# An encoder trunk on one core: the feed-forward's products in one matmul of 512 columns and one of 256, and adaLN columns taken at other places

## The chip, the cores and the metric

The kernel runs on one core of a Trainium2 chip. The metric is the device time of one execution in microseconds; the median of three runs before the change is 2146.71 us (2144.97 to 2148.68).

The engines: TensorE (PE) multiplies a stationary 128x128 weight block with up to 512 moving columns and adds into PSUM, VectorE (DVE) and ScalarE (ACT) do the elementwise work, GpSimd (POOL) a few small powers, and SyncE (SP) issues the DMAs, all on one queue. PSUM has eight banks of 512 fp32 columns in each of 128 partitions.

## The reference

Two layers over 256 tokens of width 2048. Layer 0 mixes tokens by a gated MLP, layer 1 by grouped-query attention; behind each stands a gated convolutional feed-forward. Each sub-layer is normed, and shifted, scaled and gated by columns made from a conditioning vector (adaLN):

```python
cond = silu(c)
for i in range(2):
    sh1, sc1, gt1, sh2, sc2, gt2 = split(cond @ w_ada[i] + b_ada[i], 6)
    h = rmsnorm(x, g_norm[i, 0]) * (1 + sc1) + sh1
    x = x + gt1 * (gmlp(h) if i == 0 else gqa(h))
    h = rmsnorm(x, g_norm[i, 1]) * (1 + sc2) + sh2
    x = x + gt2 * conv_ffn(h)
return rmsnorm(x, g_final)

def conv_ffn(h):                     # w_up: 2048 x 11264, w_down: 5632 x 2048
    a = h @ w_up
    a = conv_w[0]*shift(a, 1) + conv_w[1]*a + conv_w[2]*shift(a, -1) + conv_b
    g, val = split(a, 2)
    return (gelu(g) * val) @ w_down
```

Everything is fp32.

## The kernel before, in words

Activations stand transposed: 16 blocks `x[:, j, :]` of 128 features by 256 tokens. An fp32 product is made of three products of a shorter format. A weight tile (1 MB, 128x2048, by DMA) is cast on ACT into `hi` (line 188), and DVE makes the rest `lo` = w - hi (line 189), 1024 columns at a time. Activations have the same two parts, `hhi`/`hlo` for a sub-layer's input (lines 276, 277) and `fhi`/`flo` for the gated products (284, 285). `prod_b` (line 208) issues three matmuls of 256 columns into one place of PSUM: hi with hhi, hi with hlo, lo with hhi. I call these three a triple; all go through `mm` in line 205. `hi` and `lo` have five buffers each, the raw tiles five, shared by weights and adaLN columns. A whole bank holds two halves of 256 tokens: block i of the gate and its partner.

A feed-forward (`ffn`) goes through these stages. `outer` with `pfa`: seven blocks of gate and value, input blocks 0 to 7, all held at once in seven banks; their sums are parked in `part`. `pfc`: the next seven blocks over all 16 input blocks. Then `up_rest` (tile `pf`, blocks 0 to 6): the other eight input blocks, 16 triples, added to `part` (line 659). Then `up_pair` (tile `pf`, blocks 14 to 43): two weight tiles and 32 triples each. Each finished block goes to `epilogue`: two identities with scale on ACT (610), four shifted taps on DVE (613), a gelu on ACT (615), a product (616), and the split into `fhi`/`flo`. The hidden width is taken in three parts of 16, 16 and 12 blocks; behind each stands the down product `wdn` (tile `pd`): for each of 16 output blocks j, 16 or 12 triples, and a `residual` (line 291) that adds gate times sum to `x[:, j]`. In the first layer the first part is parked (`A.copy`, line 703) and added later.

An adaLN column (`ada`, line 140) is a 1 MB DMA and a DVE multiply with row sum over 128x2048; there are 192. They wait in a list. `weight` calls `pump`, which adds the stage's rate to a credit and takes a column from the list for each whole credit; `need` takes all up to one that is wanted now. The rates are `RK` for the four stages of `outer` and what follows in each layer, `RU` and `RD` in the first feed-forward's `up_pair` and `wdn`, `RW` in the attention's output product. The epilogues are not issued at once but appended to `pend`, and go when the next weight tile is issued. A scheduler then sets each engine's order by its own estimates.

After the feed-forward of layer 0 a mean square is taken (`pm_mx`, `r_mx`) on PE, DVE and POOL, then the attention's first product `pk`, 512 moving columns with the activation as the other operand, three for each pair.

## Time and profile before

| | |
|---|---|
| median of three runs | 2146.71 us |
| the profiled execution | 2148.5 us |
| its span | 2146.7 us |
| TensorE's granted clock, mean | 0.985 of 2.4 GHz |
| busy DVE, ACT | 1703.8 us, 1018.3 us |
| HBM read | 575.99 MB, 269 GB/s over the span |

A profile is one execution. Busy time is counted for each engine by itself; matmuls are pipelined, so a matmul's own 0.28 us overlaps the next, and the time it costs is the distance from start to start. The same holds on DVE and ACT to a smaller degree: I call the distance a step. The stages by their first matmuls: gated MLP to 330 us, first feed-forward 338 to 1095 us, attention 1101 to 1370 us, second feed-forward from 1380 us.

### The profile page before, as it was taken

To read this page: it belongs to the slowest core of one execution; us is meant where nothing else is said; L and a number is where in the kernel's file an instruction comes from. 1 tells how busy PE (TensorE), PEld (TensorE's weight loads), DVE (VectorE), ACT (ScalarE), POOL (GpSimd) and SP (SyncE) were. 2 spreads that over 40 slices of the span, in tenths; PEclk is the share of its full clock that TensorE was granted. 3 is DMA by queue.
4 is the path that set the end of the run, shared out by engine and by line. 5 is a ranking of instruction groups with operands and counts; after the bars stand their busy time and mean duration, and the time that the engine had idled before them with its cause. 6 is when DMAs were issued, how large, how long until landed. Compare 5 with 4: busy or idle time off the path is not lost.

```text
span 2146.7 us, 39158 instructions
## 1 busy us (share of the span) xinstructions
PE 2081.6 (97%) x16348; PEld 2026.0 (94%) x16348; DVE 1703.8 (79%) x2258; ACT 1018.3 (47%) x1484; POOL 17.4 (1%) x15
## 2 busy tenths in 40 slices
PE   6899998999999999999999999899999999999997
PEld 6778998999999999999988789899999999999997
DVE  7998999899988999889986687866978666655665
ACT  3435433446544554345445654444653445434542
POOL 0000000000000000000000000000000000000000
PEclk8999999999999999999999999899999999999999
DMA  9998898985888889988966456678558655555542
GB/s 394 404 370 331 307 382 320 366 334 214 302 343 330 331 331 330 344 323 314 338 230 225 139 196 236 217 273 310 184 194 319 231 178 192 181 190 184 182 157 95
DMA packets 85137, 580.62 MB, mean 270 GB/s; under 512 B 9952, under 2 KB 11488, under 8 KB 25056
## 3 DMA queue, kind: packets, MB, share of 16 engines
q1 hardware_dynamic: 84528, 577.93, 72.8%
q8 instruction: 128, 2.10, 0.4%
q14 instruction: 49, 0.40, 0.0%
q10 hardware_dynamic: 432, 0.20, 0.0%
HBM read 575.99 MB, written 2.10 MB: 269 GB/s over the span
## 4 chain that ended last, share of the span: by engine, by line
PE 51%; issue 37%; DVE 7%; ACT 2%; DMA 2%; POOL 0%; SPq 0%; POOLq 0%; DVEq 0%; ACTq 0%
PE pf L205 18%; PE pd L205 12%; PE po L205 4%; DVE ada L140 3%; PE pw L205 3%; PE pk L205 3%; DVE lo L189 3%; PE pq L205 3%; PE pfc L205 3%; PE pfa L205 2%; PE pub L205 1%; ACT hi L188 1%; DMA w<-in_wu 1%; PE pqo L549 1%; DMA ada<-in_wada 1%
## 5 line engine op out<-in xcount | busy, mean ns | idle before, releaser
L188 ACT CAST hi<-w 128x1024 fp32r<-128x1024 f32 x740 | 739.5, 1009 | 892.0 <-PE pf L205 353.8
L189 DVE TENSOR_TENSOR lo<-w,hi 128x1024 fp32r<-128x1024 f32 x740 | 857.4, 1169 | 323.1 <-ACT hi L188 319.8
L205 PE MATMUL pf<-hhi_f,hi 128*128 128x256 f32 x2144 | 604.3, 282 | 0.0
L205 PE MATMUL pf<-hhi_f,lo 128*128 128x256 f32 x2144 | 601.1, 280 | 0.0
L205 PE MATMUL pf<-hlo_f,hi 128*128 128x256 f32 x2144 | 600.9, 280 | 0.0
L140 DVE CUSTOM_DVE_ANT_0 ada<-ada,cond_bc,bada 128x2048 f32<-128x2048 f32 x192 | 449.6, 2346 | 37.0 <-DMA ada<-in_wada 36.9
L205 PEld LDWEIGHTS pf<-hlo_f,hi 128*128 128x128 f32 x2144 | 404.8, 189 | 0.0
L205 PEld LDWEIGHTS pf<-hhi_f,lo 128*128 128x128 f32 x2144 | 404.3, 189 | 0.0
L205 PEld LDWEIGHTS pf<-hhi_f,hi 128*128 128x128 f32 x2144 | 403.8, 188 | 0.0
L205 PE MATMUL pd<-fhi_f,lo 128*128 128x256 f32 x1408 | 394.7, 282 | 0.0
L205 PE MATMUL pd<-flo_f,hi 128*128 128x256 f32 x1408 | 393.3, 280 | 0.0
L205 PE MATMUL pd<-fhi_f,hi 128*128 128x256 f32 x1408 | 391.5, 279 | 0.2 <-ACT hi L188 0.2
L205 PEld LDWEIGHTS pd<-fhi_f,hi 128*128 128x128 f32 x1408 | 264.9, 189 | 0.4 <-ACT hi L188 0.4
L205 PEld LDWEIGHTS pd<-fhi_f,lo 128*128 128x128 f32 x1408 | 264.6, 188 | 0.2
L205 PEld LDWEIGHTS pd<-flo_f,hi 128*128 128x128 f32 x1408 | 264.5, 188 | 0.0
L205 PE MATMUL pfc<-hlo_f,hi 128*128 128x256 f32 x448 | 123.4, 283 | 1.6 <-DVE hlo_f L277 1.6
L205 PE MATMUL pfc<-hhi_f,hi 128*128 128x256 f32 x448 | 123.3, 283 | 1.1 <-ACT hi L188 1.1
L205 PE MATMUL pfc<-hhi_f,lo 128*128 128x256 f32 x448 | 113.8, 282 | 0.0
L613 DVE SCALAR_TENSOR_TENSOR t<-pf,cw,t 128x255 f32<-128x255 f32 x240 | 102.2, 475 | 0.0
L205 PEld LDWEIGHTS pfc<-hlo_f,hi 128*128 128x128 f32 x448 | 85.3, 190 | 2.0 <-DVE hlo_f L277 2.0
L205 PEld LDWEIGHTS pfc<-hhi_f,hi 128*128 128x128 f32 x448 | 85.1, 190 | 1.3 <-ACT hi L188 1.3
L205 PEld LDWEIGHTS pfc<-hhi_f,lo 128*128 128x128 f32 x448 | 79.9, 190 | 0.2 <-DVE lo L189 0.2
(194 smaller groups left out, 2809.5 us busy)
## 6 DMA issues: line engine op xcount, KB each, us to landing
ada<-in_wada SPq DMA_DIRECT2D x192, 1024.0 KB, 6.5
w<-in_wup SPq DMA_DIRECT2D x134, 1024.0 KB, 4.9
w<-in_wdn SPq DMA_DIRECT2D x64, 1024.0 KB, 4.9
w<-in_wup SPq DMA_DIRECT2D x48, 896.0 KB, 6.2
w<-in_wdn SPq DMA_DIRECT2D x32, 768.0 KB, 4.3
w<-in_wu SPq DMA_DIRECT2D x16, 1024.0 KB, 7.9
w<-in_wv SPq DMA_DIRECT2D x16, 1024.0 KB, 7.2
w<-in_wout SPq DMA_DIRECT2D x16, 1024.0 KB, 6.8
```

The costliest lines, as they stand in the source:

```text
L140: V.tensor_tensor_reduce(out=w, in0=w, in1=cond_bc, op0=ALU.mult, op1=ALU.add, scale=1.0, scalar=bada[:, l, m:m + 1], accum_out=mod[:, l, ...
L188: A.copy(hi[:, :n], w[:, c:c + n])
L189: V.tensor_tensor(out=lo[:, :n], in0=w[:, c:c + n], in1=hi[:, :n].bitcast(F32), op=ALU.subtract)
L205: T.matmul(out, lhsT=a, rhs=b, start=start, stop=stop, skip_group_check=True)
L549: T.matmul(po, lhsT=va[:, kc, g * P:(g + 1) * P], rhs=ps_[h][:, kc, :], start=kc == 0, stop=kc == TC - 1)
L613: V.scalar_tensor_tensor(out=o[:, to], in0=a[:, frm], scalar=cw[:, l, tap, n:n + 1], in1=o[:, to], op0=ALU.mult, op1=ALU.add)
```

## The change

`hhi`/`hlo` become the two halves of one tile `hh`, and `fhi`/`flo` of one tile `f`, so that both parts of an activation are 512 columns in a row. A new `prod_w` issues a matmul of `hi` with all 512 columns into a whole bank and one of `lo` with the first 256 into its first half: two matmuls for three. It is used by `up_rest`, `up_pair` and `wdn`; `outer` keeps `prod_b`. The two halves of a bank are then still to be summed. `up_pair` does this with an ACT copy of one half and a DVE sum into `ab` (function `whole`), `up_rest` with a second sum into `part`, `wdn` with a second residual, the parked part with a copy and a sum for two output blocks at once. PSUM is cut into four tiles of two banks instead of eight of one; `pfa` and `pfc` put two blocks into one tile, `wdn` two output blocks j. The rates change as the diff shows: the first attention stages get rates of their own (`RP`, `RQ`, the second set before the keys are rotated). In SP's order 138 columns are issued ahead of the attention's first weight tile instead of 160, and all 192 ahead of the first `wdn` of the second feed-forward instead of 183. The program's lines move by 2 in `mm`, and by up to 32 in `ffn`.

```diff
 HS = 20
-RK = ((0.75, 0.75, 0.75, 0.0), (0.6, 0.6, 0.6, 0.0))
-RU = 0.75
-RD = 0.85
-RW = 0.5
+RK = ((0.75, 0.75, 0.75, 0.0), (0.9, 0.9, 0.9, 0.5))
+RU = 0.55
+RD = 0.6
+RP = 0.5
+RQ = 0.5
+RW = 0.75
 RB = 5
...
     def bank(name, tag=None):
-        return cur["ps"].tile([P, 512], F32, tag=tag or cur["tag"], name=name, bufs=cur["bufs"][tag or cur["tag"]])
-    def phase(stack, name, nf, bufs={"ps": 8}, tag="ps", rt="ps"):
+        return cur["ps"].tile([P, cur["bw"]], F32, tag=tag or cur["tag"], name=name, bufs=cur["bufs"][tag or cur["tag"]])
+    def phase(stack, name, nf, bufs={"ps": 8}, tag="ps", rt="ps", bw=512):
...
                                                      space=bass.MemoryType.PSUM, reuse_waits="tile"))
-        cur["bufs"], cur["tag"], cur["rt"] = bufs, tag, rt
+        cur["bufs"], cur["tag"], cur["rt"], cur["bw"] = bufs, tag, rt, bw
         cur["f"] = stack.enter_context(tc.tile_pool(name=name + "_f", bufs=nf, reuse_waits="tile"))
...
         mm(out, wlo, xhi, False, stop)
+    def prod_w(out, w, xx, start, stop):
+        whi, wlo = w
+        mm(out, whi, xx, start, False)
+        mm(out[:, :S], wlo, xx[:, :S], False, stop)
...
     def new_h(name, step=0):
-        hts["hi"] = hbuf.tile([P, NB, S + step], F32R, tag="hhi", name=f"hhi_{name}")[:, :, :S]
-        hts["lo"] = hbuf.tile([P, NB, S + step], F32R, tag="hlo", name=f"hlo_{name}")[:, :, :S]
+        hts["x"] = hbuf.tile([P, NB, 2 * S + step], F32R, tag="hh", name=f"hh_{name}")
+        hts["hi"], hts["lo"] = hts["x"][:, :, :S], hts["x"][:, :, S:2 * S]
         return hts["hi"], hts["lo"]
...
     def split_f(name, src):
-        fbuf = cur["f"]
-        fhi = fbuf.tile([P, S + STEP], F32R, tag="fhi", name=f"fhi_{name}")[:, :S]
-        flo = fbuf.tile([P, S + STEP], F32R, tag="flo", name=f"flo_{name}")[:, :S]
+        f = cur["f"].tile([P, 2 * S + STEP], F32R, tag="f", name=f"f_{name}")
+        fhi, flo = f[:, :S], f[:, S:2 * S]
         A.copy(fhi, src)
         V.tensor_tensor(out=flo, in0=src, in1=fhi.bitcast(F32), op=ALU.subtract)
-        return fhi, flo
+        return fhi, flo, f[:, :2 * S]
...
+            state["rate"] = RP
             pk = [[bank(f"pk{t}_{n}", ("pb", "pa", "pb")[n]) for n in range(3)] for t in range(TC)]
...
         with ExitStack() as st:
-            ff = phase(st, f"ff{l}", FB)
+            ff = phase(st, f"ff{l}", FB, {"ps": 4}, bw=1024)
             R = rstd()
             hhi, hlo = new_h(f"f{l}", STEP)
+            hx = hts["x"][:, :, :2 * S]
             yacc = ff.tile([P, NB, S], F32, tag="yacc", name="yacc")
...
                 return b[:, :S], b[:, S:]
+            def banks(name):
+                two = [bank(f"{name}_{i}") for i in range((KO + 1) // 2)]
+                return [two[i // 2][:, (i % 2) * 512:(i % 2 + 1) * 512] for i in range(KO)]
+            def both(b):
+                v = b.rearrange("p (s h c) -> p s h c", s=2, h=2)
+                return v[:, :, 0, :], v[:, :, 1, :]
+            def whole(name, b):
+                t = ff.tile([P, 2 * S], F32, tag="ab", name=name, bufs=1)
+                u, v = both(b)
+                A.copy(t.rearrange("p (s c) -> p s c", s=2), v)
+                add(t, u)
+                return t
+            def add(t, u):
+                t3 = t.rearrange("p (s c) -> p s c", s=2)
+                V.tensor_tensor(out=t3, in0=u, in1=t3, op=ALU.add)
...
             state["rate"] = RK[l][0]
-            pa = [bank(f"pfa{l}_{i}") for i in range(KO)]
+            pa = banks(f"pfa{l}")
             outer(pa, range(H), wup0_d[l], 0, H - 1)
...
                 A.copy(part[:, i, :], pa[i])
-            pc = [bank(f"pfc{l}_{i}") for i in range(KO)]
+            pc = banks(f"pfc{l}")
             outer(pc, range(H), wup0_d[l, H:], 0, NB - 1)
...
                     for k in range(NB - H):
-                        prod_b(pb[:, s * S:(s + 1) * S], w((s * (NB - H) + k) * P, P), hhi[:, H + k, :],
-                               hlo[:, H + k, :], k == 0 and s == 0, k == NB - H - 1)
+                        prod_w(pb[:, s * 512:(s + 1) * 512], w((s * (NB - H) + k) * P, P), hx[:, H + k, :],
+                               k == 0, k == NB - H - 1)
                 def fin():
-                    V.tensor_tensor(out=part[:, i, :], in0=pb, in1=part[:, i, :], op=ALU.add)
+                    for b in both(pb):
+                        add(part[:, i, :], b)
                     fs[i] = epilogue(i, halves(part[:, i, :]))
...
                     for kb in range(NB):
-                        prod_b(pb[:, s * S:(s + 1) * S], w(kb * P, P), hhi[:, kb, :], hlo[:, kb, :],
-                               kb == 0 and s == 0, kb == NB - 1)
+                        prod_w(pb[:, s * 512:(s + 1) * 512], w(kb * P, P), hx[:, kb, :], kb == 0, kb == NB - 1)
                 def fin():
-                    fs[i] = epilogue(i, halves(pb))
+                    fs[i] = epilogue(i, halves(whole(f"ab{l}_{i}", pb)))
...
                     w = weight(wdn_d[l, :, off:off + nk * P], nk * P)
-                    pd = bank(f"pd{l}_{pi}_{j}")
+                    if j % 2 == 0:
+                        pd = bank(f"pd{l}_{pi}_{j}")
+                    half = pd[:, (j % 2) * 512:(j % 2 + 1) * 512]
                     for k in range(nk):
                         ks = k * P
-                        prod_b(pd[:, :S], w(ks, P), fs[base + k][0], fs[base + k][1],
-                               k == 0, k == nk - 1)
-                    def fin(j=j, pd=pd, pi=pi):
+                        prod_w(half, w(ks, P), fs[base + k][2], k == 0, k == nk - 1)
+                    def fin(j=j, pd=pd, half=half, pi=pi):
                         if pi == 0 and defer:
-                            A.copy(yacc[:, j, :], pd[:, :S])
+                            if j % 2 == 1:
+                                u, v = both(pd)
+                                A.copy(yacc[:, j - 1:j + 1, :], u)
+                                add(part[:, j // 2, :], v)
                         else:
-                            residual(l, GT2, j, pd[:, :S])
+                            residual(l, GT2, j, half[:, :S])
+                            residual(l, GT2, j, half[:, S:])
                         if pi == len(PARTS) - 1:
```

On PE the triples change, here at the end of `pfc` and the start of `pf` of the first feed-forward (the bracket tells on which engines a row waits). Before:

```order
L205 MATMUL pfc_6_3621<-hhi_f_3118,lo_1024_4492 128x256
L205 MATMUL pf_0_4632<-hhi_f_3118,hi_0_4635 128x256 [waits Activation_49]
L205 MATMUL pf_0_4632<-hlo_f_3119,hi_0_4635 128x256
L205 MATMUL pf_0_4632<-hhi_f_3118,lo_0_4636 128x256 [waits DVE_49]
L205 MATMUL pf_0_4632<-hhi_f_3118,hi_0_4635 128x256
```

Now, on PE at the same place:

```order
L207 MATMUL pfc_3_3613<-hh_f_3117,lo_1024_4484 128x256
L207 MATMUL pf_0_4617<-hh_f_3117,hi_0_4620 128x512 [waits DVE_49,Activation_49]
L207 MATMUL pf_0_4617<-hh_f_3117,lo_0_4621 128x256
L207 MATMUL pf_0_4617<-hh_f_3117,hi_0_4620 128x512
L207 MATMUL pf_0_4617<-hh_f_3117,lo_0_4621 128x256
```

Two matmuls stand in place of three, and the first of them now waits for DVE as well as for ACT: for the last tap that reads the tile `pfc_0`, whose place `pf_0` takes.

On DVE, the same place in the second feed-forward. `lo_0` and `lo_1024` are the two halves of a weight tile, `t_7` and `t_8` are epilogues of `pfc`, `yacc<-pf_0` the sum of `up_rest`. Before:

```order
L189 TENSOR_TENSOR lo_0_16229<-w_16226,hi_0_16228 128x1024
L613 SCALAR_TENSOR_TENSOR t_7_16075<-pfc_0_15173,cw,t_7_16075 128x255 x3
L613 SCALAR_TENSOR_TENSOR t_8_16088<-pfc_1_15174,cw,t_8_16088 128x255 x2
L613 SCALAR_TENSOR_TENSOR t_7_16075<-pfc_0_15173,cw,t_7_16075 128x255
L189 TENSOR_TENSOR lo_1024_16233<-w_16226,hi_1024_16232 128x1024
L613 SCALAR_TENSOR_TENSOR t_8_16088<-pfc_1_15174,cw,t_8_16088 128x255 x2
L616 TENSOR_TENSOR t_7_16075<-t_7_16075 128x256
L189 TENSOR_TENSOR lo_0_16302<-w_16299,hi_0_16301 128x1024
L616 TENSOR_TENSOR t_8_16088<-t_8_16088 128x256
L285 TENSOR_TENSOR flo_f_7_16085<-t_7_16075,fhi_f_7_16084 128x256
```

Now, on DVE at the same place:

```order
L142 ISA ada_90_14465,mod<-ada_90_14465,cond_bc,bada 128x2048
L142 ISA mod 128x1
L645 SCALAR_TENSOR_TENSOR t_7_14337<-pfc_0_13422,cw,t_7_14337 128x255 x4
L191 TENSOR_TENSOR lo_0_14471<-w_14468,hi_0_14470 128x1024
L191 TENSOR_TENSOR lo_1024_14475<-w_14468,hi_1024_14474 128x1024
L648 TENSOR_TENSOR t_7_14337<-t_7_14337 128x256
L645 SCALAR_TENSOR_TENSOR t_8_14349<-pfc_0_13422,cw,t_8_14349 128x255 x2
L191 TENSOR_TENSOR lo_0_14528<-w_14525,hi_0_14527 128x1024
L645 SCALAR_TENSOR_TENSOR t_8_14349<-pfc_0_13422,cw,t_8_14349 128x255
L292 TENSOR_TENSOR f_f_7_14346<-t_7_14337,f_f_7_14346 128x256
L645 SCALAR_TENSOR_TENSOR t_8_14349<-pfc_0_13422,cw,t_8_14349 128x255
```

A column of adaLN now stands ahead of the first tap, and `t_8` reads the same tile as `t_7` and ends eight rows later.

On DVE, the end of the first feed-forward and the step of `r_mx` to the attention. `tbqc` is a table product of the attention. Before:

```order
L235 TENSOR_TENSOR acc_mx_11308<-acc_mx_11308,sq_mx_11936 128x512
L189 TENSOR_TENSOR lo_0_12120<-w_12117,hi_0_12119 128x1024
L235 TENSOR_TENSOR acc_mx_11308<-acc_mx_11308,sq_mx_11990 128x256
L189 TENSOR_TENSOR lo_1024_12124<-w_12117,hi_1024_12123 128x512
L291 SCALAR_TENSOR_TENSOR x<-pd_2_15_11993,mod,x 128x256
L189 TENSOR_TENSOR lo_0_12152<-w_12149,hi_0_12151 128x1024
L250 TENSOR_SCALAR r_mx_12046<-pm_mx_12045 128x2
L445 TENSOR_TENSOR tbqc<-tbqc,gbqc 128x256
```

Now, on DVE at the same place:

```order
L191 TENSOR_TENSOR lo_1024_10329<-w_10322,hi_1024_10328 128x512
L243 TENSOR_TENSOR acc_mx_9686<-acc_mx_9686,sq_mx_10162 128x512
L298 SCALAR_TENSOR_TENSOR x<-pd_2_14_10165,mod,x 128x256
L191 TENSOR_TENSOR lo_0_10357<-w_10354,hi_0_10356 128x1024
L298 SCALAR_TENSOR_TENSOR x<-pd_2_14_10165,mod,x 128x256
L243 TENSOR_TENSOR acc_mx_9686<-acc_mx_9686,sq_mx_10205 128x256
L142 ISA ada_44_10453,mod<-ada_44_10453,cond_bc,bada 128x2048
L142 ISA mod 128x1
L452 TENSOR_TENSOR tbqc<-tbqc,gbqc 128x256
L258 TENSOR_SCALAR r_mx_10249<-pm_mx_10248 128x2
```

There are two residuals for the last tile, and the column `ada_44` and the table product have moved ahead of `r_mx`.

## Rows read from the trace of the kernel before

**Rows 1.** Page, part 1: busy us (share of span), instructions.

```profile
PE 2081.6 (97%) x16348; PEld 2026.0 (94%) x16348; DVE 1703.8 (79%) x2258; ACT 1018.3 (47%) x1484; POOL 17.4 (1%) x15
```

**Rows 2.** Chain of waits: start us, us, engine, tile, line, matmuls.

```profile
464.99 85.18 PE pf L205 x720
...
1100.80 67.11 PE pk L205 x288
```

**Rows 3.** Windows: us, busy PE, PEld, DVE, ACT, POOL, clock, DMA share, GB/s.

```profile
500.00:550.00 50.00, 50.00 (x424) 50.00 (x424) 47.93 (x77) 32.04 (x53) 0.00 (x0) 1.00 0.68 247
...
1030.00:1095.00 65.00, 64.81 (x547) 64.37 (x547) 61.30 (x84) 29.70 (x40) 0.00 (x0) 1.00 0.92 346
...
1110.00:1160.00 50.00, 50.00 (x222) 41.42 (x221) 31.08 (x44) 22.88 (x34) 0.00 (x0) 1.00 0.64 218
...
1503.00:1545.00 42.00, 42.00 (x358) 42.00 (x357) 39.62 (x71) 28.87 (x48) 0.00 (x0) 1.00 0.51 182
```

**Rows 4.** Timeline, PE, first `pf`: start us, us, engine, line, names.

```profile
479.72 0.28 PE L205 MATMUL pf<-hhi_f,hi 128*128 128x256 f32 x1
...
481.96 0.28 PE L205 MATMUL pf<-hlo_f,hi 128*128 128x256 f32 x1
```

**Rows 5.** Timeline, PE, attention keys `pk`, 512 columns.

```profile
1123.78 0.39 PE L205 MATMUL pk<-hi,hhi_b 128*128 128x512 f32 x1
...
1126.95 0.39 PE L205 MATMUL pk<-hi,hhi_b 128*128 128x512 f32 x1
```

**Rows 6.** Groups by form: shapes, count, busy us, mean ns, idle before.

```profile
L205 PE MATMUL pf<-hhi_f,hi 128*128 128x256 f32 x2144 | 604.3, 282 | 0.0
...
L205 PE MATMUL pd<-fhi_f,hi 128*128 128x256 f32 x1408 | 391.5, 279 | 0.2 <-ACT hi L188 0.2
...
L291 DVE SCALAR_TENSOR_TENSOR x<-pd,mod,x 128x256 f32<-128x256 f32 x80 | 38.3, 482 | 24.1 <-PE pd L205 22.5
...
L641 ACT COPY yacc<-pfa 128x512 f32<-128x512 f32 x14 | 7.3, 612 | 3.8 <-PE pfa L205 3.8
```

**Rows 7.** Timeline, DVE, from `pfc` to `pf`, first feed-forward.

```profile
455.54 2.35 DVE L140 CUSTOM_DVE_ANT_0 ada<-ada,cond_bc,bada 128x2048 f32<-128x2048 f32 x1
...
457.81 0.48 DVE L277 SCALAR_TENSOR_TENSOR hlo_f<-ht_f,mod,hhi_f 128x256 fp32r<-128x256 f32 x1
...
462.89 2.96 DVE L613 SCALAR_TENSOR_TENSOR t<-pfc,cw,t 128x255 f32<-128x255 f32 x7 [0.32 <-ACT t L610]
465.76 1.21 DVE L189 TENSOR_TENSOR lo<-w,hi 128x1024 fp32r<-128x1024 f32 x1
466.90 0.48 DVE L613 SCALAR_TENSOR_TENSOR t<-pfc,cw,t 128x255 f32<-128x255 f32 x1
467.29 1.22 DVE L189 TENSOR_TENSOR lo<-w,hi 128x1024 fp32r<-128x1024 f32 x1
...
471.03 0.68 DVE L659 TENSOR_TENSOR yacc<-pf,yacc 128x512 f32<-128x512 f32 x1
471.63 0.41 DVE L616 TENSOR_TENSOR t<-t 128x256 f32<-128x256 f32 x1
471.96 1.22 DVE L189 TENSOR_TENSOR lo<-w,hi 128x1024 fp32r<-128x1024 f32 x1
```

**Rows 8.** Timeline, DVE and PE, same place, second feed-forward.

```profile
1501.13 2.43 DVE L613 SCALAR_TENSOR_TENSOR t<-pfc,cw,t 128x255 f32<-128x255 f32 x6
...
1503.80 0.28 PE L205 MATMUL pf<-hhi_f,hi 128*128 128x256 f32 x1
```

**Rows 9.** Timeline, DVE, from feed-forward to attention.

```profile
1097.41 0.15 DVE L250 TENSOR_SCALAR r_mx<-pm_mx 128x2 f32<-128x2 f32 x1
1098.17 0.43 DVE L445 TENSOR_TENSOR tbqc<-tbqc,gbqc 128x256 f32<-128x256 f32 x1 [0.60 <-DMA gbqc<-in_gq]
```

**Rows 10.** Timeline, DVE, from attention to second feed-forward.

```profile
1371.25 2.35 DVE L140 CUSTOM_DVE_ANT_0 ada<-ada,cond_bc,bada 128x2048 f32<-128x2048 f32 x1 [1.58 <-DMA ada<-in_wada]
```

More of the change, by code (lines that the diff above doesn't have):

```diff
@@ L122 @@
     cur["ps"] = c_st.enter_context(tc.tile_pool(name="c_ps", bufs=2, space=bass.MemoryType.PSUM, reuse_waits="tile"))
-    cur["tag"], cur["bufs"] = "ps", {"ps": 2}
+    cur["tag"], cur["bufs"], cur["bw"] = "ps", {"ps": 2}, 512
     def spread(out, col):
@@ L483, in rope @@
                 return rot, ss
+            state["rate"] = RQ
             krot, rk = rope("k", [pk[t][0] for t in range(TC)], "k")
```

## The prediction

> **What bounds the kernel now.** I read the page's busy table first, then the chain, then the table by windows, then single steps. TensorE (PE) is busy for 97% of the span, VectorE (DVE) for 79% [rows 1]. The chain of waits names long unbroken PE pieces inside the feed-forwards: 720 matmuls of `pf` in 85.18 us without a foreign wait [rows 2]. By windows, PE has 50 of 50 us in the middle of a feed-forward, and within 0.2 us so it is in every window that I took inside their bodies; but DVE there stands at 47.9 of 50, 61.3 of 65 and 39.6 of 42 [rows 3]. So the bodies are bound by how fast PE steps from matmul to matmul, with a DVE close behind: less PE work helps at full value, more DVE work is free only while the last 5 to 10% of cover holds. The busy time of a matmul (0.28 us) overlaps its neighbours; the price is the step from start to start.
>
> **Step 1, fewer matmuls.** Before, each triple is three matmuls of 256 columns; now it is one of 512 and one of 256. Steps: from 479.72 to 481.96 there are 19, so 117.9 ns each [rows 4]; for 512 columns from 1123.78 to 1126.95 there are 14, so 226.4 ns [rows 5]. The columns are the same; what goes is what a matmul costs beside its columns: 2 x 117.9 - 226.4 = 9.4 ns. Triples changed: 2144 of `pf` and 1408 of `pd` [rows 6], 3552 in all; 3552 x 9.4 ns = **-33 us**. `pfa` and `pfc` keep the old product. Bounds: the window 1110:1160 has 222 steps in 50 us, 225.2 ns [rows 3], which makes -38; the piece of the chain with 288 of `pk` in 67.11 us gives 233 ns, and against 118.3 (85.18 / 720) [rows 2] only 3.6 ns, which makes -13. I take the undisturbed steps, which lie nearest to what runs inside a feed-forward.
>
> The Trainium skill (TensorE: Matmul & The Clock Gate, Back-to-back issue gap) gives the gap of an isolated warm matmul as its columns over 2.4 GHz plus about 2.5 ns, so that a merged matmul saves 2.5 ns and not 9.4; by that the term would be an estimated -9 us. The rows disagree: 117.9 ns is 11 above 256 / 2.4, 226.4 is 13 above 512 / 2.4. I go by the rows, and keep the case of a small saving below.
>
> **Step 2, more DVE and ACT work.** The halves of a product now lie in two places and are summed later. DVE steps [rows 7]: a `lo` of 1024 columns 1.14 us (467.29 less 466.90 gives 0.39 for a tap, 466.90 less 465.76 gives 1.14), a 128x512 sum 0.60, a 128x256 product 0.33, a column of adaLN 2.27. New: 60 + 14 + 8 sums of 0.60 and 80 more residuals of 0.41: 82 us of DVE over two feed-forwards of some 750 us each, and 60 copies of 0.61 on ACT [rows 6], which is half idle. A pair of `pf` then needs on DVE four `lo` (4.56), four taps (1.6), two products (0.7), the sum (0.6) and 1.1 columns (2.5): 10.0 of the 11.0 us that PE needs for its 32 triples at 344 ns. In the body of `pf` I cost it at nothing; the lower rate in the first feed-forward (0.55 for 0.75) is what pays for it. If that cover went, each pair would be some 1 us late, 15 to 30 us in all.
>
> **Step 3, the start of `pf`.** The PSUM tiles are now four of two banks, all held by `pfc` when it ends. The first `pf` therefore waits until DVE has taken the last tap from the first tile, and this comes behind DVE work that no matmul waited for before: three taps, `lo`, a tap, `lo`, a product, `lo`, four taps and a product: 8 x 0.41 + 3 x 1.14 + 2 x 0.33 = 7.4 us from the first tap at 462.89 [rows 7]; `pfc` ends at 464.99 [rows 2]. So **+5.3 us** in the first feed-forward; the later `pf` (5.5 us of PE each) cover the following tiles. In the second the rate there goes from 0 to 0.5, and a column of 2.27 us stands in front of the taps, another behind `t_8`. The taps begin 2.7 us before `pfc` ends in the trace [rows 8]; with the column in front I take 1.5: `pf_0` waits 5.9. `pf_1` waits for the last tap of `t_10`, 7.0 us of DVE rows on, while PE works 5.5: 1.5. `pf_2` waits for the second sum of `pf_0`: 9.2 us of rows (two `lo`, a column, the taps of two tiles, two sums, one more `lo`) against 5.5: 3.7. `pf_3` and `pf_4` 0.4 each. Together **+11.9**. Low end for both boundaries 5 (sums and taps as early as PE ends), high end 25.
>
> **Step 4, `pd` in halves of a tile.** Two output blocks share a tile, so PE's order is first halves of two tiles, then second halves, and each second half waits for both residuals of the first half, 80 waits less those of the parked part. Between lies one block, 12 or 16 triples, 4.1 or 5.5 us of PE. DVE makes it where it has slack; in the last part of the first feed-forward it does not: 16 blocks need 66.5 us of DVE (1.74 `lo`, 0.82 residuals, 0.3 sums each, and nine columns) in 66 us of PE. Before, it was 61.3 of 65 busy [rows 3]. Behind a waiting second half stand all later blocks. I take **+4.5**, from 1 (only the block that lies next to its own half, in both layers) to 10.
>
> **Step 5, into the attention.** Before the step of `r_mx`, DVE's order now holds two residuals for each of the last blocks, the column `ada_44` and the table product of `tbqc`, whose gain was waited for until 1098.17, after `r_mx` at 1097.41 [rows 9]. The DMA of `ada_44` stands on SP's queue behind the first weight tiles' buffers, and the gain's DMA behind it. One column and a residual are 2.7 us, and the chain through POOL to `pk` hangs on it: **+3.5**, 2 to 6.
>
> **Step 6, columns taken later.** 15 more columns fall into the attention, 34 us of DVE in 270 us, where it stands at 31 of 50 in `pk` [rows 3]. The chains of softmax are short and pass through DVE; a column in front of a maximum delays it by up to 2.3 us, but PE has the next `pq` to do: **+3**, 0 to 10. At the end of `wo` one column no longer holds the last residuals, behind its DMA for 1.58 us at 1371.25 [rows 10]: **-1.5**. The doubled residual at both ends: +0.8.
>
> **Sum.** -33 + 5.3 + 11.9 + 4.5 + 3.5 + 3 - 1.5 + 0.8 = -5.2 on the profiled execution of 2148.5 (span 2146.7 and 1.8 around it): 2143. The median of the runs stands 1.8 below the profiled one: 2141.5. Of the terms the waits at the second boundary rest on the longest walk with all waits in a row, and a tap or sum that comes early takes from all that follow; I shift by 1.5 for it: **2140 us**.
>
> **Rivals.**
> A. The waits are hidden, the saving stays: `pf` gets its tile with one DVE step of delay, the residuals are in time. For it: PE never waited in these bodies, and the order puts residuals early. Against it: the DVE rows ahead of `t_8` are real work. -33 and some 10 of waits: about 2124.
> B. Slower by DVE. At 10.0 of 11.0 us a pair, and 66.5 of 66 in the last `pd`, any column whose DMA is late (1.58 us in rows 10) makes DVE miss a half; a whole tile is two banks, so PE stops for it at once. It decides from the point where DVE's need of a pair passes 11 us, ten percent above my walk; 60 pairs at 0.4 us and boundaries at 25 give +24 + 25 + 11 - 33 = +27 at the far end, +10 half way: about 2157.
> C. Slower by a small saving. If a step of 512 columns in the feed-forward costs the 233 ns of the chain piece [rows 2], the saving is 13 and the waits of 28 stay: +15, about 2161. The two-step rows speak against it. (By the Trainium skill's 2.5 ns, same page and section as above, it would be an estimated 4 us later still.)
> D. It does not do what it says in time: saving and waits cancel within what a measurement can tell, 2142.4 to 2151 (0.2% either way, about the least this kernel's measurement tells from no change).
>
> **Chances.** Forecast, 2133 to 2142: 0.37. A: 0.19. D: 0.25. B: 0.13. C: 0.06. Faster by over 0.2%: 0.37 + 0.19 = 0.56, of which 0.01 goes to D's edge: 0.55. Within: 0.26. Slower: 0.19. Range, to leave out half of A's far end and the far ends of B and C: 2120 to 2157; the forecast's own is 2133 to 2148.
>
> **What would show it.** Steps of 344 to 346 ns for a pair of matmuls in `pf` and `pd` (354 would deny step 1). At the end of `pfc`, PE gaps of 5 us, and in the second layer four gaps of 12 in sum, released by DVE; none would make A right. In the bodies no DVE-released gaps; many short ones before `pf` say B. In the last `pd` gaps released by residuals. An `r_mx` 3 us later against the last matmul of `pd`. I would be wrong above all if PE waits in the body of `pf`, or if the boundaries cost nothing.

## The result and the profile after

The changed kernel takes 2185.44 us (median of four runs, 2180.49 to 2189.07) against 2147.69 us before (four runs as well): ratio 1.017, 95% interval 1.0157 to 1.0184, slower by 38 us. I had forecast 2140 with a range of 2120 to 2157. The profiled execution took 2189.07 us, its span is 2187.3 us.

The stages, from the first matmul of one to the first or last of the next (us, from the timelines of PE). The last four columns are runs that are told below.

| | before | after | rates alone | one-bank | clean ends | clean ends, low |
|---|---|---|---|---|---|---|
| first feed-forward (`pfa` to last `pd`) | 757.0 | 768.2 | 755.6 | 755.3 | 759.2 | 757.2 |
| step into the attention | 5.8 | 10.4 | 12.3 | 14.4 | 6.6 | 5.9 |
| attention (`pk` to last `pw`) | 269.6 | 282.0 | 279.7 | 278.4 | 271.5 | 273.5 |
| step into the second feed-forward | 11.6 | 13.6 | 9.4 | 10.0 | 7.7 | 7.7 |
| second feed-forward | 751.3 | 760.3 | 751.0 | 750.5 | 743.1 | 743.6 |
| before `pfa`, and the end | 351.4 | 352.9 | 352.6 | 352.3 | 351.9 | 352.1 |

From the first feed-forward on every stage is longer, by 2 to 12 us; no single one holds the loss.

The page's first part of the changed kernel, to be held against [rows 1]:

```profile
PE 2082.4 (95%) x12796; PEld 1860.8 (85%) x12796; DVE 1787.6 (82%) x2420; ACT 1056.2 (48%) x1536; POOL 20.8 (1%) x15
```

PE has 3552 matmuls less and the same busy time; its share falls to 95%. The windows (columns as in [rows 3]):

```profile
1030.00:1095.00 65.00, 59.15 (x313) 50.34 (x312) 54.88 (x76) 26.96 (x37) 0.00 (x0) 0.92 0.74 264
1117.00:1190.00 73.00, 70.51 (x294) 56.12 (x294) 53.87 (x77) 33.02 (x60) 0.00 (x0) 0.97 0.67 249
1540.00:1580.00 40.00, 36.33 (x193) 31.21 (x192) 39.27 (x65) 21.75 (x35) 0.00 (x0) 0.93 0.67 238
1700.00:1800.00 100.00, 100.00 (x572) 87.25 (x572) 66.48 (x89) 50.89 (x68) 0.00 (x0) 1.00 0.53 186
```

In the body of a feed-forward (1700 to 1800) PE is full as before. In the last `pd` of the first feed-forward, in `pk` and at the start of the second `pf` it is not, and there the granted clock lies at 0.92 to 0.97, where [rows 3] has 1.00 (for `pk` a part of that is the window, which takes in its start; the start ran at the lower level before the change too): after a wait PE's first matmuls run at the lower of its two levels. One sees it in the steps behind the first gap, and in the body beside it what the merged product costs. PE's timeline at the end of `pfc`, then in the body of `pf`:

```profile
463.90 0.28 PE L207 MATMUL pfc<-hh_f,lo 128*128 128x256 f32 x1
470.33 0.77 PE L207 MATMUL pf<-hh_f,hi 128*128 128x512 f32 x1 [6.15 <-DVE t L645]
470.89 0.42 PE L207 MATMUL pf<-hh_f,lo 128*128 128x256 f32 x1
471.11 0.63 PE L207 MATMUL pf<-hh_f,hi 128*128 128x512 f32 x1
...
700.04 0.39 PE L207 MATMUL pf<-hh_f,hi 128*128 128x512 f32 x1
...
703.90 0.39 PE L207 MATMUL pf<-hh_f,hi 128*128 128x512 f32 x1
```

From 470.89 to 471.11 a matmul of 256 columns takes 0.22 us, where one in the body takes 0.12 (the level of 1.2 GHz against 2.4). From 700.04 to 703.90 there are 11 pairs: 350.9 ns each. Over the pairs of `pf`, without the waits and the slower steps behind them, the mean step is 233.0 ns behind a matmul of 512 columns and 117.8 behind one of 256; in the kernel before it is 118.3 for each of three. The pair saves some 4 ns, not 9.4.

DVE at the start of `pf`, first feed-forward, beside [rows 7]:

```profile
462.89 1.26 DVE L645 SCALAR_TENSOR_TENSOR t<-pfc,cw,t 128x255 f32<-128x255 f32 x3
464.07 1.22 DVE L191 TENSOR_TENSOR lo<-w,hi 128x1024 fp32r<-128x1024 f32 x1
465.20 0.48 DVE L645 SCALAR_TENSOR_TENSOR t<-pfc,cw,t 128x255 f32<-128x255 f32 x1
465.59 1.22 DVE L191 TENSOR_TENSOR lo<-w,hi 128x1024 fp32r<-128x1024 f32 x1
466.73 0.42 DVE L648 TENSOR_TENSOR t<-t 128x256 f32<-128x256 f32 x1
467.06 1.22 DVE L191 TENSOR_TENSOR lo<-w,hi 128x1024 fp32r<-128x1024 f32 x1
468.20 0.87 DVE L645 SCALAR_TENSOR_TENSOR t<-pfc,cw,t 128x255 f32<-128x255 f32 x2
468.98 0.42 DVE L292 TENSOR_TENSOR f_f<-t,f_f 128x256 fp32r<-128x256 f32 x1
469.31 0.87 DVE L645 SCALAR_TENSOR_TENSOR t<-pfc,cw,t 128x255 f32<-128x255 f32 x2
```

This is the walk of step 3, row for row: the last tap of the first tile ends at 470.2, and `pf` starts at 470.33. In the second feed-forward, beside [rows 8], DVE's timeline:

```profile
1528.35 2.35 DVE L142 CUSTOM_DVE_ANT_0 ada<-ada,cond_bc,bada 128x2048 f32<-128x2048 f32 x1
...
1530.84 1.66 DVE L645 SCALAR_TENSOR_TENSOR t<-pfc,cw,t 128x255 f32<-128x255 f32 x4
...
1538.16 0.48 DVE L645 SCALAR_TENSOR_TENSOR t<-pfc,cw,t 128x255 f32<-128x255 f32 x1
1538.55 2.35 DVE L142 CUSTOM_DVE_ANT_0 ada<-ada,cond_bc,bada 128x2048 f32<-128x2048 f32 x1
...
1547.33 2.35 DVE L142 CUSTOM_DVE_ANT_0 ada<-ada,cond_bc,bada 128x2048 f32<-128x2048 f32 x1
```

PE's table of waits there (engine, tile, line, releaser: us in all, times, longest):

```profile
PE pf L207 <- DVE t L645: 5.9, 2, 5.5
PE pf L207 <- DVE yacc L635: 3.3, 1, 3.3
```

A column stands before the first tap, and two more before the taps and sums that free the next tiles. PE waits 5.5 us for a tap, and 3.3 for a sum into `part`.

From 1018 to 1118 us, around the last `pd` of the first feed-forward, PE's and DVE's rows in the same table:

```profile
PE pd L207 <- DVE f_f L292: 3.8, 1, 3.8
...
PE pd L207 <- DVE x L298: 2.7, 2, 1.7
...
DVE ada L142 <- DMA ada<-in_wada: 8.6, 7, 3.4
```

The longest of PE's waits, in its timeline:

```profile
1034.22 0.28 PE L207 MATMUL pd<-f_f,lo 128*128 128x256 f32 x1
1038.33 0.79 PE L207 MATMUL pd<-f_f,hi 128*128 128x512 f32 x1 [3.82 <-DVE f_f L292]
```

DVE's rows that lead to it, and the longest of its own waits:

```profile
1034.10 2.35 DVE L142 CUSTOM_DVE_ANT_0 ada<-ada,cond_bc,bada 128x2048 f32<-128x2048 f32 x1 [0.80 <-DMA ada<-in_wada]
...
1037.85 0.42 DVE L292 TENSOR_TENSOR f_f<-t,f_f 128x256 fp32r<-128x256 f32 x1
...
1046.42 2.35 DVE L142 CUSTOM_DVE_ANT_0 ada<-ada,cond_bc,bada 128x2048 f32<-128x2048 f32 x1 [3.40 <-DMA ada<-in_wada]
```

A column stands ahead of the split (`f_f`, line 292) of the last gated block, and PE waits for that split. Later DVE stands still for 3.4 us with a column whose DMA has not landed; everything behind it in its order waits as well, but PE has work then and stops next at 1077.5. The attention, DVE's timeline before its first transposes:

```profile
1206.12 0.68 DVE L479 TENSOR_TENSOR rotq<-pk,tbqc 128x512 f32<-128x512 f32 x1
...
1211.64 2.35 DVE L142 CUSTOM_DVE_ANT_0 ada<-ada,cond_bc,bada 128x2048 f32<-128x2048 f32 x1 [0.63 <-DMA ada<-in_wada]
...
1213.92 0.69 DVE L488 TENSOR_TENSOR rotq<-rotq,swq 128x512 f32<-128x512 f32 x1
```

And PE's waits there:

```profile
PE pqo L523 <- DVE rotq L488: 6.9, 2, 4.0
```

The sum that ends the rotated query (`rotq`, line 488) stands right behind a column that waits for its DMA; PE waits for such a sum twice, 6.9 us in all. Most of the rest is lost in `pk`, which takes 71.9 us for 66.7. Between the first `pk` and the last `pw` DVE now takes 27 columns, where it took 11.

### The profile page after: what moved, and what is told of

Its sections match the earlier page's. It is cut to its first block, busy times and chain, and to the rows that moved or that the text cites. A ratio compares the mean times of both kernels' runs of the same rounds, so it can differ in the third digit from the quotient of the medians.

```text
span 2187.3 us, 32289 instructions
## 1 busy us (share of the span) xinstructions
PE 2082.4 (95%) x12796; PEld 1860.8 (85%) x12796; DVE 1787.6 (82%) x2420; ACT 1056.2 (48%) x1536; POOL 20.8 (1%) x15
## 4 chain that ended last, share of the span: by engine, by line
PE 45%; issue 37%; DVE 10%; DMA 6%; ACT 1%; POOL 0%; DVEq 0%; SPq 0%; POOLq 0%; ACTq 0%
PE pf L207 17%; PE pd L207 11%; DMA ada<-in_wada 4%; PE po L207 4%; DVE ada L142 4%; DVE lo L191 4%; PE pw L207 3%; PE pfc L207 3%; PE pfa L207 2%; PE pub L207 2%; PE pq L207 2%; ACT hi L190 1%; PE pqo L558 1%; DMA w<-in_wu 1%; PE pv L207 0%
## 5 line engine op out<-in xcount | busy, mean ns | idle before, releaser
L207 PE MATMUL pf<-hh_f,hi 128*128 128x512 f32 x2144 | 757.0, 397 | 15.3 <-DVE t L645 12.1
L207 PE MATMUL pf<-hh_f,lo 128*128 128x256 f32 x2144 | 603.1, 281 | 0.0
L207 PE MATMUL pd<-f_f,hi 128*128 128x512 f32 x1408 | 497.7, 397 | 10.1 <-DVE f_f L292 5.4
L207 PEld LDWEIGHTS pf<-hh_f,hi 128*128 128x128 f32 x2144 | 404.9, 189 | 113.4 <-ACT t L642 7.0
L207 PEld LDWEIGHTS pf<-hh_f,lo 128*128 128x128 f32 x2144 | 405.8, 189 | 0.0
L207 PE MATMUL pd<-f_f,lo 128*128 128x256 f32 x1408 | 395.5, 282 | 0.0
L207 PEld LDWEIGHTS pd<-f_f,hi 128*128 128x128 f32 x1408 | 266.7, 190 | 73.6 <-DVE f_f L292 6.0
L207 PEld LDWEIGHTS pd<-f_f,lo 128*128 128x128 f32 x1408 | 267.4, 190 | 0.8 <-DVE lo L191 0.3
L207 PE MATMUL pfc<-hh_f,hi 128*128 128x256 f32 x896 | 156.9, 282 | 1.9 <-DVE hh_f L285 1.4
L207 PEld LDWEIGHTS pfc<-hh_f,hi 128*128 128x128 f32 x896 | 134.8, 189 | 2.5 <-DVE hh_f L285 1.8
```

The lines of the kernel that those rows point to most:

```text
L207: T.matmul(out, lhsT=a, rhs=b, start=start, stop=stop, skip_group_check=True)
```

## The experiments

**The two parts of the change apart.** The first run takes the new products with the old rates, the second the old products with the new rates:

```diff
-RK = ((0.75, 0.75, 0.75, 0.0), (0.9, 0.9, 0.9, 0.5)); RU = 0.55; RD = 0.6; RP = RQ = 0.5; RW = 0.75
+RK = ((0.75, 0.75, 0.75, 0.0), (0.6, 0.6, 0.6, 0.0)); RU = 0.75; RD = 0.85; RP = RQ = 0.0; RW = 0.5
```

> The changed kernel with the rates of before (RK, RU, RD, RW as before, none in the first attention stages), all else of the change kept. Theory R (the rates cost most: columns taken in the attention hold its DVE chains): the 12 us lost in the attention, about 5 at its two ends and 7 of the 12.6 at the second pf boundary come back, about 2163 us, pk again 67 us long. Theory H (the halves' sums on DVE and the shared tiles cost most): DVE in the first feed-forward, which now has its old columns and the new sums, passes what PE needs (about 11.4 of 11.2 us a pair), so the attention gains 12 but the first feed-forward loses 20 or more: about 2190 us or above.

Measured: 2185.48 us, ratio 1.0171 (1.0156 to 1.0186), the same as the changed kernel. The attention is back at 271.1 us and the second feed-forward at 753.3, but the first takes 786.0, with gaps in two of its down products. So theory H holds for the first feed-forward and theory R for the rest; on the total H missed by 5 us and R by 22. The step into the attention is back at 5.7 us, and at the second `pf` boundary, with no columns there, 6.3 of 12.8 us are left.

> The kernel before with the new rates alone (old products, old tiles, old epilogue). Theory R: the attention and its ends lose what they lose in the changed kernel, 12 to 20 us: about 2163 us. Theory H: DVE has slack without the sums, columns in the attention are mostly hidden: 2147 to 2152 us.

Measured: 2160.42 us, ratio 1.0054 (1.0039 to 1.0069): +12 us from the rates alone. The feed-forwards don't change (755.6 and 751.0); the loss is 10 us in the attention and 6 in the step to it. DVE's waits in that run from 1095 to 1300 us:

```profile
DVE ada L142 <- DMA ada<-in_wada: 19.8, 11, 4.3
```

The same row of the kernel before:

```profile
DVE ada L140 <- DMA ada<-in_wada: 1.3, 4, 0.5
```

Eleven columns come before their data, and each holds a DVE on which the rotation and the softmax hang. Theory R. Whether these waits or the columns' own 2.3 us weigh more, no run parts. The second `pf` starts without a gap here: the columns alone cost that boundary nothing, the new product in shared tiles without columns 6.3 us, both together 12.8.

**Is it the alternation of 512 and 256 columns that costs 233 ns?** In the next run all products with `hi` of a weight tile come first, then all with `lo`:

```diff
-            prod_w(pb[...], w(kb * P, P), hx[:, kb, :], kb == 0, kb == NB - 1)
+        for i, ((whi, wlo), xx) in enumerate(zip(ws, xs)):
+            mm(out, whi, xx, i == 0, False)
+        for i, ((whi, wlo), xx) in enumerate(zip(ws, xs)):
+            mm(out[:, :S], wlo, xx[:, :S], False, i == len(ws) - 1)
```

> The changed kernel with each product's matmuls grouped: first all of hi with 512 columns, then all of lo with 256. Theory A (a matmul of 512 columns costs 233 ns instead of 227 because it alternates with one of 256): steps of 226 to 227 ns inside the groups, a pair 344 to 345 ns, 3552 x 6 ns = 21 us less than the changed kernel, about 2164 us. Theory M (the moving operand, activations out of the wide tile, costs it): steps of 233 ns in the groups too, the time within 5 us of the changed kernel's 2185.

Measured: 2193.98 us. In `pf` the step from one matmul of 512 columns to the next of its kind is 232.6 ns, from 256 to 256 it is 119.0. Theory A falls; the operands remain. The time is 8.5 us above the changed kernel, where theory M had it within 5: PE's waits behind 800 us in the first feed-forward grew by 6 us; why stays open. The trace had a hint: in the second feed-forward's `up_pair` the step after a 512-column matmul depends on the input block kb alone, and it comes back in every weight tile (mean ns for kb = 0 to 7, and the same for 8 to 15):

```
232.3 234.3 233.4 235.9 231.7 231.7 235.8 229.2
```

Two runs change the distance from block to block, and with it where each begins:

```diff
-STEP = 8
+STEP = 4      (the other run: STEP = 0)
```

> The changed kernel with 4 columns of padding behind each activation pair instead of 8, so that the address of a block moves on by 2064 bytes instead of 2080; nothing else. Theory P (where a moving block begins sets the step, 229 to 236 ns for 512 columns): the pattern of steps over the 16 input blocks changes, with a period of 16 blocks or another mean; Theory W (the place of the weight block inside its tile sets it): the same eight steps as before, 229 to 236 in the same order.

> The changed kernel with no padding, so that each block begins a multiple of 2048 bytes on. Theory P: one step for all 16 input blocks, whatever it is between 226 and 240 ns. Theory W: the same eight steps, 229 to 236 ns.

Measured (one execution of each, 2185.89 and 2187.93 us). With 4 the pattern has 16 different places, 228.5 to 240.9 ns, the same in both feed-forwards. With 0 the block makes no difference any more: the mean step in `up_pair` is 230.7 ns for every block in the first feed-forward and 236.4 in the second. PE's timeline of the last of these, first and second feed-forward, 11 and 12 pairs apart:

```profile
700.15 0.39 PE L207 MATMUL pf<-hh_f,hi 128*128 128x512 f32 x1
...
703.96 0.39 PE L207 MATMUL pf<-hh_f,hi 128*128 128x512 f32 x1
...
1749.91 0.40 PE L207 MATMUL pf<-hh_f,hi 128*128 128x512 f32 x1
1750.15 0.28 PE L207 MATMUL pf<-hh_f,lo 128*128 128x256 f32 x1
1750.26 0.40 PE L207 MATMUL pf<-hh_f,hi 128*128 128x512 f32 x1
1750.49 0.28 PE L207 MATMUL pf<-hh_f,lo 128*128 128x256 f32 x1
...
1754.15 0.40 PE L207 MATMUL pf<-hh_f,hi 128*128 128x512 f32 x1
```

346.4 and 353.3 ns for a pair. Theory W falls, since the weights lie where they lay: the distance between the moving blocks makes the pattern. Theory P is not shown in full. It had one step for all blocks, but in the second feed-forward single steps go 241, 236, 233 ns in turn, three pairs and not a block long (0.24 us from 1749.91, 0.23 from 1750.26), and the two feed-forwards differ though the pool of the tile, `hbuf`, has one buffer. So something besides the block's own start takes part. Nor does the distance explain the mean: it is 233.0 with 8, 233.9 with 4, and 230.7 and 236.4 with 0, always above the 226.4 of the weights that move in `pk` [rows 5]. Why an activation with 512 columns steps more slowly there, by its place or by either operand, was not tried and stays open.

**The shared tiles.** First the down product alone gets one tile for each output block:

```diff
-                    if j % 2 == 0:
-                        pd = bank(f"pd{l}_{pi}_{j}")
-                    half = pd[:, (j % 2) * 512:(j % 2 + 1) * 512]
+                    pd = bank(f"pd{l}_{pi}_{j}")
+                    half = pd[:, :512]
```

> The changed kernel with a PSUM tile of its own for each output block of the down product (half of each tile unused), so that no second half waits for a first; the parked part is then copied and summed block by block. Theory H1 (waits on the shared tile make the loss in the last down products, 12 us in the first and 4.6 in the second feed-forward): 8 to 14 us less, about 2174 us. Rival H2 (there it is the DVE's queue, a column ahead of the split of the last gated block, and PE waits for that whatever the tile): within 4 us of 2185, the 4 us gap before the last pd still there.

Measured: 2176.02 us, 9 us less. The last `pd` takes 68.7 us (79.6 in the changed kernel, 67.1 is what its steps make) and 67.2 in the second feed-forward (71.7). H1. The 4 us gap that the rival had laid to DVE's queue went too, though DVE's rows up to the split of the last gated block are the same and end at the same time:

```profile
1033.89 2.35 DVE L142 CUSTOM_DVE_ANT_0 ada<-ada,cond_bc,bada 128x2048 f32<-128x2048 f32 x1 [0.70 <-DMA ada<-in_wada]
...
1037.64 0.42 DVE L292 TENSOR_TENSOR f_f<-t,f_f 128x256 fp32r<-128x256 f32 x1
```

What changed is PE's work in hand. In the changed kernel it has 44 matmuls before it stops for that split, 22 pairs, as many as two output blocks have for the 11 gated blocks before the last; here it has 97 before its first stop. Then every tile is one bank:

```diff
-            ff = phase(st, f"ff{l}", FB, {"ps": 4}, bw=1024)
+            ff = phase(st, f"ff{l}", FB)
-                pb = bank(f"pf{l}_{i}")
+                pb = [bank(f"pf{l}_{i}_{s}") for s in range(2)]
...
+                for s in range(2):
+                    u, v = both(b[s])
+                    A.copy(t[:, s * S:(s + 1) * S], v)
+                    add(t[:, s * S:(s + 1) * S], u)
```

> The changed kernel with eight PSUM tiles of one bank again: each half of a gate-and-value block has a bank of its own, each output block of the down product one; the sums are then made half by half (two of 256 columns for one of 512, some 10 us more DVE in all). New rates kept. Theory T (sharing a tile of two banks makes the waits at the start of pf, 5.4 and 13 us, and most of those of the last pd, 12 and 4.6 us): the first pf starts without a gap, and 18 to 30 us go, about 2158 us. Rival Q (DVE's queue is full, whoever shares): waits move to lo or to the taps and at most 8 us go, 2177 us or above.

Measured: 2161.85 us, ratio 1.0061 (1.0045 to 1.0076), 23.6 us less than the changed kernel. PE's timeline at the end of `pfc`:

```profile
464.44 0.28 PE L207 MATMUL pfc<-hh_f,lo 128*128 128x256 f32 x1
464.56 0.39 PE L207 MATMUL pf<-hh_f,hi 128*128 128x512 f32 x1
```

The gap of 6.4 us is gone, and of 12.8 us in the second feed-forward 2.6 are left. Theory T. The run costs as much as the rates alone cost the old kernel, 13 us above it, and loses it in the same places; in the first down products a new gap of 3 us appears each time, released by the split of a gated block.

**Columns placed elsewhere.** The next run adds rates of none in the attention's first stages:

```diff
+RK = ((0.75, 0.75, 0.75, 0.0), (0.9, 0.9, 0.9, 0.0)); RU = 0.65; RD = 0.7; RP = RQ = 0.0; RW = 0.6
...
+            if l == 1:
+                state["rate"] = 0.75
```

> As the run with one-bank tiles, and rates RK[1] = (.9, .9, .9, 0), RU .65, RD .7, RW .6, none in the first attention stages, 0.75 in the second feed-forward from its first full pf block on. Theory R+T (columns in the attention cost the 12.4 us that the rates alone cost the kernel before; the tile costs the rest): another 10 to 14 us less than one-bank tiles alone, about 2146 us or below, the kernel before matched or beaten by up to 10. Rival Q: the first feed-forward with more columns falls behind its DVE by 10 us or more, in the last pd above all, and nothing is won over one-bank tiles alone.

Measured: 2166.87 us. The attention came back (270.5 us), as R+T has it, but 17 us of gaps opened in the second feed-forward's first down product, released by late splits, where the rate of 0.75 had put columns ahead of them. Rival Q has it that nothing is won over one-bank tiles alone, and so it was, though not in the place that it named: the columns had only been moved ahead of another chain. So the second feed-forward's first part was parked as well, which lets the last 16 columns wait, and the last five blocks before the attention were freed of columns. Two runs, the new and the old product with that same placing:

```diff
+RU = 0.6; RD = 0.65
...
-                if l == 0 and pi > 0:
+                if pi > 0:
                     state["rate"] = RU
...
+                    if l == 0:
+                        state["rate"] = 0.0 if pi == 2 and j >= 11 else RD
...
-    ffn(1, lambda: rstd_bcast("ff1", True), "fin", False)
+    ffn(1, lambda: rstd_bcast("ff1", True), "fin", True)
```

> One-bank tiles and the merged product, with the columns moved away from where they were seen to hurt: none in the first attention stages and in the last five blocks of the first feed-forward's last down product, rates .6 and .65 in its body, .6 in the output product, and the second feed-forward's first part parked too (its residual added later), so that its gate columns may wait for its second third. If columns in front of short chains are what was left of the loss: attention 266 us as before, the step into it 6 to 8 us, 14 us less from the steps of 351 for 355 ns, some 4 us of gaps in the first down product: about 2143 us. If the doubled sums on DVE cost by themselves: 2152 us or above.

> The kernel before (three matmuls, its tiles and epilogue) with the same placing of the columns and the second parked part. It differs from the run beside it by the merged product and its halves alone. If the merged product is worth its 14 us in the bodies and loses a part to its sums: 3 to 10 us slower than that run, and within 5 us of the kernel before. If the halves cost more than 14 us wherever the columns stand: faster than that run.

Measured: 2150.54 us with the new product, ratio 1.0009 (1.0001 to 1.0018), and 2159.14 with the old, 1.005 (1.0037 to 1.0062). The merged product with its doubled sums is thus worth 8.6 us under this placing, in the span of one execution of each 12.7 us (2147.9 and 2160.6), 7.5 of them in the second feed-forward (743.2 and 750.7). My numbers for both runs were off: the new product stands between its two marks (2143 and 2152), the old one 11 us above the kernel before and not within 5, so that this placing is a bad one for it. With the new product this placing lost 5 us in the step into the second feed-forward (16.6 for 11.6) and 5 in the attention (274.9 for 269.6); why it lost the latter stays open. The last pair takes the columns out of there (`RK[1][0]` = 0) and spreads them over the stages before:

```diff
+RK = ((0.75, 0.75, 0.75, 0.0), (0.0, 0.9, 0.9, 0.0))
+RU = 0.7; RD = 0.75; RW = 0.75      (the other run: RU = 0.65; RD = 0.7; RW = 0.9)
```

> As the best new placing, with no column left in the chains at the attention's two ends: none in pfa of the second feed-forward (rate 0), so the first feed-forward carries more (.7 and .75) and the output product .75. If a column ahead of the square sums is what made the second end 16.6 us long instead of 11.6: that end 11 us or less and about 2144 us, 4 us under the kernel before. If DVE in the first feed-forward's bodies is too full at these rates: gaps in its down products and 2150 us or above.

> The same with a lighter first feed-forward (.65 and .7) and more columns in the output product (.9). If the first feed-forward's DVE decides: a few us under the run beside it, about 2142 us; if the output product's residuals are late instead: the second end longer, 2148 us or above.

Measured: 2141.88 us, ratio 0.9968 (0.9957 to 0.9979), and 2140.55 us, 0.9962 (0.9949 to 0.9974). Both beat the kernel before, by 6 and 8 us; whether the first feed-forward's lighter load tells, the two can't say, since their intervals overlap. The step into the second feed-forward is 7.7 us in both. The old product was not run with this last placing, so how much of the 6 to 8 us belongs to the product is not shown; the 8.6 us above hold for the placing before it. The second's page, first part:

```profile
PE 2072.0 (97%) x12796; PEld 1855.8 (87%) x12796; DVE 1794.5 (84%) x2516; ACT 1062.5 (50%) x1620; POOL 17.7 (1%) x15
```

And the waits of PE for a late split that are left from 540 to 1110 us:

```profile
PE pd L207 <- DVE f_f L292: 5.4, 2, 4.4
```

DVE is busier than in the changed kernel (84% for 82%) and PE waits less: it was not the sum of DVE's work alone that hurt, but what stood in front of what.

## Why the prediction was wrong

Three terms of the sum failed: the saving of step 1 (-33 for -15 us), the shared halves of step 4 (4.5 for 17) and the columns of step 6 (1.5 for 14.4). They make 43.5 of the 46.5 us between the forecast sum and the measured one. The terms as I wrote them add up to -5.5 and not -5.2, which changes nothing here.

**Step 1, the saving: twice too large.** I carried the step of 512 columns from `pk` [rows 5] into the feed-forward. There a weight moves and steps at 226.4 ns; here an activation does, and steps at 233.0 on the mean; the runs leave open why. A pair takes 351 ns, between the 344 to 346 that I had named as the sign of a full saving and the 354 that would have denied it. A down product of 256 triples takes 89.37 us for 90.44, 4.2 ns for each; 3552 at that are 15 us, where the sum has 33. The price of rival C (13 us) was near, but by luck: the 233 ns that I read out of [rows 2] for it came from the start of `pk`, whose first steps ran at the lower clock (0.43 us from the start at 1101.39 to the next at 1101.82), and not from a matmul that costs more. The Trainium skill's gap (TensorE: Matmul & The Clock Gate, Back-to-back issue gap), 2.5 ns beside the columns, gives about 216 ns for 512 and an estimated saving of 9 us; the trace agrees with neither its 216 nor my 226.4.

**Step 2, the body: right.** From 470 to 1018 us PE's only wait is the one for the first `pf`, and in the 100 us window of the second feed-forward PE is full and the pairs step at 351 ns; the sums cost nothing there. That the lower rate pays for them, as I wrote, the run with the old rates shows: with 20 columns more in the first feed-forward it takes 18 us longer.

**Step 3, the start of `pf`: right in mechanism, a little small.** 5.3 was 7.8 (6.3 of waiting, the rest slower steps at the low clock behind it), 11.9 was 12.8, counted alike. The run with one-bank tiles shows the cause: 17.6 of these 20.6 us go with the sharing.

**Step 4, the halves of a tile: four times too small.** 4.5 predicted, 12.5 and 4.5 measured, 17 in all. I priced second halves that wait for residuals; in the first feed-forward these waits are 2.7 us. The longest, 3.8 us, is for the split of the last gated block, which I did not have: with two output blocks to a tile PE had work for two blocks only until that split came, behind a column. Slower steps at the low clock stand behind each wait. I weighed DVE's sum of work (66.5 against 66 us) and did not walk its order against PE's. A late DVE alone is not the cause: with the rates alone DVE waits 7.5 us for columns' DMAs in the same down product and PE never stops, and with its own tile for each block the split comes as late and 1.6 of the 12.5 us are left. Rival B named this mechanism, a late column and a tile of two banks; it did not come in the body of `pf`, as I had it, but in the last `pd`.

**Step 5, into the attention: right in size** (3.5 for 4.6), with the column and the late square sums in front of `r_mx`. With the old rates, without that column, the step is 5.7 us as before.

**Step 6, columns taken later: the overlap was wrong.** 3 predicted for the attention, 12.4 measured, and +2.0 for -1.5 behind it. The run with the rates alone shows 10 of them without any new product. I counted 34 us of DVE work against 270 us and a DVE at 31 of 50, and wrote that PE has the next `pq` to do. It had not: PE waits 6.9 us for the rotated query, a wait that is not there before the change, and `pk` takes 5 us more. The columns wait for their DMAs (19.8 us in the run with the rates alone, 1.3 before) and stand in front of chains behind which PE has nothing else.

Sum: -14.9 (step 1) + 7.8 + 12.8 (step 3) + 17.0 (step 4) + 4.6 (step 5) + 12.4 + 2.0 (step 6) + 1.3 (behind the last `pd`) = +43.0, less 2.0 for `pfa` and `pfc`, 1 us shorter in each feed-forward: 41.0, where the spans differ by 40.6 us.

## What to carry to other kernels

A matmul of the same width stepped at 226 ns in one product and at 233 in another, so a price for a wider matmul is read from one with the same operands, or bounded from the worst row. Work that is put on an engine with slack is not free when that engine's order is fixed: look at what stands behind it, and whether the waiting engine has other work in hand. And a tile that two results share is freed by the later one; one-bank tiles gave back 24 of the 38 us lost here.

## What the runs showed of the hardware

The step of a 512-column float32r matmul with an activation as the moving operand varied between 228 and 241 ns. With moving blocks 2080 bytes apart it repeated over 8 blocks, with 2064 over 16, with the same means by block in both feed-forwards; with 2048 it did not depend on the block, and was 230.7 ns on the mean in the first feed-forward and 236.4 in the second, there in a cycle of three (241, 236, 233). With a weight as the moving operand, in `pk` before the change, it was 226.4. After waits of some us the first matmuls ran at the lower clock (0.22 us for 256 columns from 470.89 to 471.11): the mean granted clock of a stretch of 65 us in which PE was idle for 5.9 us was 0.92.
